# Rope as a delayed task, other delays in the solve, the fourth head's projections moved, products behind a norm run per token group, and w_mod moved into the FFN output

## The chip, the cores and the metric

The kernel runs on one core of one Trainium2 chip. The metric is the device time of one execution in microseconds. The engines are TensorE (PE; PEld is its weight load), VectorE (DVE), ScalarE (ACT), GpSimd (POOL) and SyncE (SP), which here only issues DMA transfers.

## The reference

A two-layer bidirectional encoder, run on two groups of 256 tokens with shared weights; the model width is 1024. The kernel holds both groups side by side as 512 token columns.

```python
def encoder_layer(x, c, cos, sin, p):
    sh1, sc1, gt1, sh2, sc2, gt2 = split(silu(c) @ p['w_mod'] + p['b_mod'], 6)
    h = rmsnorm(x, p['ln1_g']) * (1 + sc1) + sh1
    (q_down, kv_down, rg_x, rg_gate, gdn_qkv, gdn_z,
     gdn_alpha, gdn_beta, gates) = split_cols(h @ p['w_in'], IN_SPLITS)
    o_mla = mla_branch(...)     # latent attention, 8 heads, 32 rotary columns each
    o_rg  = rglru_branch(...)   # gated linear recurrence, both directions
    o_gdn = gdn_branch(...)     # chunked gated DeltaNet, 4 heads, both directions
    mixed = sum over n of sigmoid(gates[n]) * (o_n @ p['w_branch'][n])
    x = x + gt1 * (mixed @ p['w_out'])
    h2 = rmsnorm(x, p['ln2_g']) * (1 + sc2) + sh2
    u_lin, u_gate = split(dwconv_centred(h2 @ p['ffn_w_up'], ...), 2)
    return x + gt2 * ((silu(u_gate) * u_lin) @ p['ffn_w_down'])
# twice, then a final rmsnorm
```

In a DeltaNet head each chunk of 64 tokens needs the inverse of a unit lower triangular matrix, and then a short recurrence over the chunks.

## The kernel before

**Products.** Every large product takes float32 operands split into a high and a low part: `mm3` (L410) issues high by high, high by low and low by high into one PSUM bank. The weights lie in DRAM in *units* of 128x128, in the order of use, eight units to a *chunk* of 512 KB. `split_chunk` (L382) prefetches the chunk two further on, casts a loaded chunk to its high part on ACT (`wh`) and subtracts on DVE (`wl`); `unit` (L395) hands out one unit after the other and calls it six units ahead of a chunk's first use. There are four load buffers and two of each part. `gemm` (L416) makes one output row of 128 with all 512 token columns, or with 256 of one group; `gemms` (L425) makes three or six rows together. A row takes a bank of the PSUM pool `mm` (3 banks, L246); everything small, and three rows of every `gemms`, a bank of the pool `aux` (5 banks, L247).

**Order.** PE and SP run in the order in which the program is written; DVE, ACT and POOL are ordered by the framework. The program is written out by a planner: `Driver` (L141) counts a time of PE from the products issued. The list `BRANCHES` (L33) and `jobs` (L43) give the order of the large products; side tasks are generators that yield a delay of the table `SLACK` (L61) or an event, and after every unit `poll` runs those that are due. `until` waits for an event: it runs due tasks, then tasks from the list `spare`, and else moves the time on.

**Jobs.** `in6` makes the low-rank projections; `uq`, `uk`, `uv` the queries, keys and values of the attention; `gq.h`, `gk.h`, `gv.h`, `z.h` the DeltaNet projections of head h; `x`, `g`, `b` the recurrence; `gate.b.d` and `br.b.d` gate and output row d of branch b; then come the output projection (`out`), the FFN's `up` rows and the `down` rows.

**Rope.** `query` (L793) rotates rows 4 and 5 of the queries on DVE and at once writes on SP the transfer `drope` to DRAM and two transfers back into `Qt`; the event `ev_q`, for which the attention waits, follows 1.5 us later.

**The solve.** For each head `solve` (L1339) makes the decay and Gram products, writes the diagonal blocks out (`cb`, transfer `dl`), reads them into `Lb`, inverts them on POOL by 30 small steps (`xt`, `X`), writes them out (`dx`) and reads them into `W`. `combine` (L1452) then builds the inverse (`gdn_l`) and runs the recurrence (`gdn_rec`, `gdn_o`); it ends with a norm over `ssq` and `spread`. `combine` of a head begins after that of the head before (`ev_free`), and `gq.2` and `gq.3` wait for `ev_free` of two heads before.

**Norms.** `Norm` (L594) collects the squares as rows are finished. `scale` (L616) sums them on PE, takes the root on DVE and spreads it on PE into an `aux` bank that it holds while `modulated` (L582) reads it: DVE multiplies (`hn`, four buffers), ACT scales and shifts, POOL copies to the high part `hh`, DVE subtracts to the low part `hl`. Before the FFN and before the second layer the kernel waits for both groups' norms, runs the spare w_mod products meanwhile, makes all sixteen half tiles and then goes on with `up3` or `in6` over 512 columns. The last two output rows (`out` 6 and 7) and the last `down` row are made per group, group 0 first. The w_mod products of the second layer's first norm come in two lots (`ahead`, L1063): one paced through the `down` rows, one as spare work.

Of the kernel before, what the change touches and what calls it, by code (L numbers as in the profile page):

```python
# [1 line left out]

# [1 line left out]

# [21 lines left out]
AHEAD = 6  # L26
UC = 8

E2 = 0

# [6 lines left out]
    g.2 x.3 b.2.0 gate.1.2 b.2.1 gq.2 gk.2 gv.2 gate.1.3 g.3 b.3.0 gate.1.4 b.3.1 gate.1.5 gate.1.6  # L37
# [14 lines left out]

SIZE = {"in6": 48, "gq": 8, "gk": 8, "gv": 8, "uq": 3, "uk": 2, "pad": 2, "uv": 8,
        "gate": 8, "br": 4, "x": 8, "g": 8, "b": 2, "z": 8, "out3": 24, "out": 8, "up3": 24, "up": 8,
        "down": NFF, "close": 0, "mid": 0, "close2": 0}
JOBS = jobs()
NU = sum(SIZE[j[0]] for j in JOBS)
NCH = -(-NU // UC)
# [2 lines left out]
SLACK = {  # L61
    "modev": 0.7, "att_s": 3.2, "att_t": 1.8, "att_e": 1.0, "low_rank": 11.8, "low_rank_out": 152.5, "mla": 0.2,
# [3 lines left out]
    "rg_all": 16.0, "ssq": 6.5, "kq": 8.0, "norm": 2.8, "normed": 17.0, "mod1": 8.0, "mod2": 8.0,  # L66
    "kd": 0.1, "start": 0.6, "diag2": 4.6, "cq": 2.1, "lr_diag": 5.3, "diag": 30.4}


# [165 lines left out]
def _body(es, tc, nc, xT, cT, wall, wmod, pvec, fng, cst, rope, xinit, yT, dbg):  # L235
# [156 lines left out]
            sub(wl, raw, f32(wh))  # L392
            pieces[at] = (wh, wl)

    def unit():  # L395
        l, u = state["l"], state["u"]
        if u % UC == 0:
            split_chunk((l, u // UC))
            state["piece"] = pieces.pop((l, u // UC))
        elif (u + AHEAD) % UC == 0 and u + AHEAD < NU:  # L400
# [6 lines left out]
    def bank():  # L407
        return mm.tile([P, T], F32, name="mm_" + state["job"], tag="mm")

    def mm3(ps, w, x, first, last):  # L410
        PE.matmul(ps, w[0], x[0], start=first, stop=False)
        PE.matmul(ps, w[0], x[1], start=False, stop=False)
        PE.matmul(ps, w[1], x[0], start=False, stop=last)


    def gemm(xs, g=2):  # L416
# [177 lines left out]

    class Norm:
# [111 lines left out]

    for l in range(depth):
        state.update(l=l, u=0, job="in6")
        first = gemms(hs(h) if l else first_h(), 6)  # L710
        if not l:
            start.close()
            setup(0)
        pr = prm[l]

# [77 lines left out]
        def query(j):  # L793
            if j == 0:
                drv.until(ev_cq)
            ps = gemm(cq)
            if j < 4:
                A.activation(Qt[0:64, 2 * j, :], ps[0:64], AF.Copy, scale=96.0 ** -0.5)
                A.activation(Qt[0:64, 2 * j + 1, :], ps[64:128], AF.Copy, scale=96.0 ** -0.5)
                return  # L800
            cosq, sinq = rep2(rt_[:, 0, :]), rep2(rt_[:, 1, :])
            if j == 4:
                lr["rope"] = mp.tile([P, 4, T], F32, name="rope", tag="Vt")
            ab = lr["rope"][:, 2 * j - 8:2 * j - 6, :]
            mul(halves(ab[:, 0, :]), halves(ps), cosq)
            mul(halves(ab[:, 1, :]), halves(ps), sinq)
            if j == 5:
                x, y = lr["rope"][:, 0:2, :], ab
                sub(x[:, 0, :], x[:, 0, :], y[:, 1, :])
                add(x[:, 1, :], x[:, 1, :], y[:, 0, :])  # L810
                dr = dp.tile([P, 2, T], F32, name="drope", tag="drope")
                nc.sync.dma_start(dr, x)
                for e in range(2):
                    nc.sync.dma_start(Qt[64 + 16 * e:80 + 16 * e], dr.rearrange("(h p) e t -> e p h t", p=16)[e])
                ev_q.set(SLACK["rope"])

        def values():
            Vt = lr["Vt"] = mp.tile([P, 4, T], F32, name="Vt", tag="Vt")
# [182 lines left out]
                debug(f"x1_{d}_{l}", t)  # L1001


        def early(l, which, xs, sq, ks, h, pool):
            yield SLACK["norm"]
            yield from sq.scale(0)
            r = sq.r[0]
            for k in ks:
                x = xs[k]
                modulated(l, which, x[0] if isinstance(x, tuple) else x, r, k, 0, h, pool, 4)  # L1010


        def result(xs, sq, g):
# [47 lines left out]
            return tuple(half)  # L1061

        def ahead():  # L1063
            yield from modulation(l + 1, ((0, 1),), SLACK["mod2"], next_raw, 8)
            drv.spare.append([0.0, modulation(l + 1, ((2, 3),), 0.0, next_raw, 8)])


        last = l + 1 == depth
        for job in JOBS:
# [91 lines left out]
                    out_row(ps, d, 2)  # L1161
            elif k == "out":
                d, g = ix
                out_row(gemm(ms_, g), d, g)
                if (d, g) == (7, 0):
                    h2 = {}
                    drv.spawn(early(l, 1, x1, sq, range(E2), h2, op_))
                elif (d, g) == (7, 1):
                    wait(SLACK["norm"])
                    for us in sq.scale(1):  # L1170
                        wait(us)
                    for k in range(8):
                        for g in ((1,) if k < E2 else (0, 1)):
                            modulated(l, 1, x1[k], sq.r[g], k, g, h2, op_, 4)
                    wait(SLACK["normed"])
                    drv.drain_spare()
                    fill(op_, 2016)
                    ostack.close()
                    rstack.close()
                    fstack = ExitStack()  # L1180
                    fp = fstack.enter_context(tc.tile_pool(name="ffn", bufs=1))
            elif k == "up3":
                for n, ps in enumerate(gemms(hs(h2), 3)):
                    up(ps, n)
            elif k == "up":
                up(gemm(hs(h2)), ix[0])
            elif k == "down":
# [6 lines left out]
                        drv.spawn(ahead())  # L1194
                ps = gemm(acts, g)
                t = x1[d]
                for e in ((0, 1) if g == 2 else (g,)):
                    c = GS[e]
                    stt(t[:, c], ps[:, c], modA[:, 3, d, e:e + 1], t[:, c], ALU.mult, ALU.add)
                    if not last:  # L1200
                        nc.scalar.dma_start(xdram[:, d, c], t[:, c])
                sq.put(t, d, g)
                if g:
                    debug(f"x2_{d}_{l}", t)
                if last and d < 7:
                    A.activation(t, t, AF.Copy, scale=fg[:, d:d + 1])
                if (d, g) == (7, 0):
                    h = {}
                    drv.spawn(result(x1, sq, 0) if last else early(l + 1, 0, x1, sq, (), h, fp))
        if not last:  # L1210
            wait(SLACK["norm"])
            for us in sq.scale(1):
                wait(us)
            drv.drain_spare()
            for k in range(8):
                for g in range(2):
                    modulated(l + 1, 0, x1[k], sq.r[g], k, g, h, fp, 4)
            wait(SLACK["normed"])
        else:
            drv.spawn(result(x1, sq, 1))  # L1220
            drv.finish()
        fstack.close()


class GDN:
# [398 lines left out]
def pack(inp):  # L1624
# [11 lines left out]
    for l in range(depth):  # L1636
# [26 lines left out]
        for k, *ix in JOBS:  # L1663
# [14 lines left out]
            elif k == "up3":  # L1678
                w = side(up)
            elif k == "up":  # L1680
                w = up[ix[0]]
            elif SIZE[k] and k != "pad":
                w = seg[k][ix[0]]
            n = SIZE[k]
            if n and k != "pad":
                wall[l, u:u + n] = w.reshape(n, P, P)
            u += n

# [46 lines left out]
```

## Time and profile before

| | |
|---|---|
| median of 3 runs | 2016.12 us (2014.07 to 2019.35) |
| profiled execution | 2019.3 us, span 2017.5 us |
| PE busy | 1949.8 us, 97%, 11563 products |
| PEld busy | 1564.2 us, 78% |
| DVE busy | 1235.5 us, 61% |
| ACT busy | 823.9 us, 41% |
| POOL busy | 258.0 us, 13% |
| mean granted clock of PE | 0.986 |
| DMA | 231.44 MB, 115 GB/s |

Times are in microseconds from the start of the span. A view of waits says who waited for whom and how long in total; a timeline lists instructions with start and length, and in brackets the idle time ahead of one and what ended it; in a view of windows each engine has its busy time and, in brackets, its instructions, and the granted clock is a share of full speed. Lines such as L298 can be those of a helper, so the tile's name tells more than the line. Products are pipelined, so the length of one is more than the distance to the next.

### The profile page before, as it was taken

How to read it: one execution, taken by the hardware profiler on the slowest of the kernel's cores; microseconds unless marked ns; L12 is line 12 of the kernel's file. 1: busy time of each engine (PE TensorE's matmuls, PEld its weight loads, DVE VectorE, ACT ScalarE, POOL GpSimd, SP SyncE). 2: the span in 40 equal slices, each digit the busy share in tenths (PEclk: the TensorE clock that was granted, in tenths of full speed). 3: DMA queues.
4: the chain of work that ended last, by engine and by line, in shares of the span. 5: the costliest groups of instructions: out<-in, count | busy, mean ns of one | idle time of the engine just before them, and what ended most of it. 6: DMA issues, size and time to landing. Idle time of an engine off the chain costs nothing.

```text
span 2017.5 us, 29521 instructions
## 1 busy us (share of the span) xinstructions
PE 1949.8 (97%) x11563; PEld 1564.2 (78%) x11563; DVE 1235.5 (61%) x2324; ACT 823.9 (41%) x1275; POOL 258.0 (13%) x511
## 2 busy tenths in 40 slices
PE   9999999989999999999999999999898999999998
PEld 5777777768777888887877777777687888888887
DVE  5765776755456766652357758776553677676534
ACT  3444366523323544432234534655222344444322
POOL 1100162132200100000011004513130010000000
PEclk9999999999999999999999999999999999999999
DMA  8131443443325233353533123443432533333233
GB/s 318 63 115 53 111 129 113 122 129 94 92 97 186 95 94 104 95 178 106 192 121 94 63 74 113 120 141 110 124 76 74 214 100 94 96 96 100 94 97 102
DMA packets 141851, 231.44 MB, mean 115 GB/s; under 512 B 79760, under 2 KB 84240, under 8 KB 141712
## 3 DMA queue, kind: packets, MB, share of 16 engines
q1 hardware_dynamic: 136240, 221.95, 35.4%
q10 hardware_dynamic: 5472, 7.61, 1.1%
q8 instruction: 91, 1.49, 0.3%
q14 instruction: 48, 0.39, 0.1%
HBM read 221.66 MB, written 7.86 MB: 114 GB/s over the span
## 4 chain that ended last, share of the span: by engine, by line
PE 82%; DVE 5%; POOL 4%; DMA 4%; issue 2%; ACT 2%; SPq 2%; POOLq 0%; ACTq 0%; DVEq 0%
PE mm_up L220 24%; PE mm_down L220 12%; PE mm_gate L220 10%; PE mm_br L220 6%; PE mm_in L220 3%; PE mm_out L220 3%; PE mm_gk L220 2%; PE mod L220 2%; PE mm_gq L220 2%; POOL xt L292 2%; PE mm_gv L220 2%; POOL X L298 2%; PE att_s L220 1%; PE gdn_rec L220 1%; PE gdn_l L220 1%
## 5 line engine op out<-in xcount | busy, mean ns | idle before, releaser
L298 DVE TENSOR_TENSOR wl<-raw,wh 128x1024 fp32r<-128x1024 f32 x304 | 374.0, 1232 | 322.2 <-ACT wh L391 321.6
L391 ACT CAST wh<-raw 128x1024 fp32r<-128x1024 f32 x304 | 318.3, 1049 | 485.3 <-PE mm_down L220 127.9
L220 PE MATMUL mm_up<-hh,wh 128*128 128x512 f32 x704 | 275.8, 392 | 3.4 <-POOL hh L308 3.4
L220 PE MATMUL mm_up<-hl,wh 128*128 128x512 f32 x704 | 275.3, 391 | 0.0
L220 PE MATMUL mm_up<-hh,wl 128*128 128x512 f32 x704 | 275.1, 391 | 0.0
L301 DVE SCALAR_TENSOR_TENSOR cv<-mm_up,pv,cv 128x510 f32<-128x510 f32 x176 | 131.2, 748 | 61.3 <-ACT cv L571 58.0
L220 PE MATMUL mm_gate<-hh,wh 128*128 128x512 f32 x384 | 163.8, 427 | 0.3
L220 PEld LDWEIGHTS mm_up<-hh,wh 128*128 128x128 f32 x704 | 133.0, 189 | 31.6 <-POOL hh L308 3.9
L220 PEld LDWEIGHTS mm_up<-hl,wh 128*128 128x128 f32 x704 | 133.0, 189 | 28.0 <-DVE hl L298 0.3
L220 PEld LDWEIGHTS mm_up<-hh,wl 128*128 128x128 f32 x704 | 133.0, 189 | 27.6
L220 PE MATMUL mm_gate<-hl,wh 128*128 128x512 f32 x384 | 151.2, 394 | 0.0
L220 PE MATMUL mm_gate<-hh,wl 128*128 128x512 f32 x384 | 151.0, 393 | 0.0
L220 PE MATMUL mm_down<-ah,wh 128*128 128x512 f32 (+1 forms) x396 | 145.9, 369 | 0.0
L220 PE MATMUL mm_down<-ah,wl 128*128 128x512 f32 (+1 forms) x396 | 144.9, 366 | 0.6 <-DVE wl L298 0.6
L220 PE MATMUL mm_down<-al,wh 128*128 128x512 f32 (+1 forms) x396 | 144.7, 365 | 0.0
L308 POOL TENSOR_SCALAR hh<-hn 128x256 fp32r<-128x256 f32 x64 | 34.4, 549 | 663.8 <-ACT hn L588 661.2
L571 ACT ACTIVATE cv<-mm_up,pv 128x512 f32<-128x512 f32 x88 | 68.5, 780 | 88.9 <-PE mm_up L220 88.9
L220 PEld LDWEIGHTS mm_gate<-hh,wh 128*128 128x128 f32 x384 | 73.0, 190 | 22.2 <-issue 7.4
L220 PEld LDWEIGHTS mm_down<-ah,wh 128*128 128x128 f32 x396 | 74.7, 189 | 15.0 <-issue 3.3
L220 PEld LDWEIGHTS mm_gate<-hh,wl 128*128 128x128 f32 x384 | 72.7, 189 | 16.4
L220 PEld LDWEIGHTS mm_down<-ah,wl 128*128 128x128 f32 x396 | 74.7, 189 | 12.9 <-DVE wl L298 0.8
L220 PEld LDWEIGHTS mm_down<-al,wh 128*128 128x128 f32 x396 | 74.7, 189 | 11.9
(386 smaller groups left out, 3836.9 us busy)
## 6 DMA issues: line engine op xcount, KB each, us to landing
raw<-in_wall_dram SPq DMA_DIRECT2D x304, 512.0 KB, 3.6
raw<-in_wmod_dram SPq DMA_DIRECT2D x48, 512.0 KB, 3.6
mraw<-in_wmod_dram SPq DMA_DIRECT2D x16, 512.0 KB, 9.9
oraw<-in_wmod_dram SPq DMA_DIRECT2D x16, 512.0 KB, 6.6
hraw<-in_wmod_dram SPq DMA_DIRECT2D x32, 256.0 KB, 5.4
x<-in_xT_dram SPq DMA_DIRECT2D x8, 256.0 KB, 6.1
W<-dx SPq DMA_DIRECT2D x32, 64.0 KB, 3.0
xr<-in_xT_dram ACTq DMA_DIRECT2D x8, 256.0 KB, 3.7
```

Source lines behind the costliest of these rows:

```text
L220: return self.pe.matmul(out, lhsT, rhs, **kw)
L292: (eng or V).tensor_tensor(out, a, b, ALU.mult)
L298: (eng or V).tensor_tensor(out, a, b, ALU.subtract)
L301: V.scalar_tensor_tensor(out, a, s, b, op0, op1)
L308: G.tensor_scalar(hi, x, 1.0, 0.0, ALU.mult, ALU.add)
L391: A.copy(wh, raw)
L571: A.activation(dst, ps, AF.Identity, bias=bias, scale=w[lo])
```

## The change

- `BRANCHES`: `gq.3`, `gk.3` and `gv.3` stand directly behind `b.3.1`; the gates, branch rows and `z` around them are in another order.
- Delays of the solve: cb 4 to 5, dl 2.5 to 4, X 18 to 17, dx 3 to 5, W 3 to 4.
- Rope: the transfers are written by a spawned task, `drope` 6 us after the rotation, `Qt` 3 later, the event 4 later.
- Output rows 5, 6 and 7 (before: 6 and 7) are made per group, all of group 0 first; two jobs `pad2` fill the last chunk up, so that `up3` begins with a chunk.
- The new `gemms_behind` stands for `gemms` at `up3` and at `in6` of the second layer: its first 16 units are run over group 0's columns after that group's event, then over group 1's after the other event, and the rest over all columns. The task `behind` makes each group's norm and half tiles and sets the event.
- `modulated` has two instructions of DVE and one of ACT.
- The w_mod products of the second layer's first norm are all paced through the `down` rows, every 5 us (before: half of them, every 8 us).
- The last rows' additions for group 1 have priority, and the stores to `xdram` are written after the squares.

```diff
-    g.2 x.3 ... gate.1.4 b.3.1 gate.1.5 gate.1.6
-    br.1.0 br.1.1 gq.3 br.1.2 z.0 gk.3 br.1.3 gate.2.0 gv.3 gate.2.1 br.1.4 z.1 gate.2.2 br.1.5
-    gate.1.7 z.2 br.1.6 gate.2.3 gate.2.4 br.1.7 gate.2.5 z.3 gate.2.6 mid gate.2.7 br.2.0 br.2.1
+    g.2 x.3 ... gate.1.4 b.3.1 gq.3 gk.3 gv.3
+    gate.1.5 z.0 br.1.0 br.1.1 gate.1.6 br.1.2 br.1.3 gate.1.7 z.1 br.1.4 br.1.5 br.1.6 br.1.7 gate.2.0
+    gate.2.1 z.2 gate.2.2 gate.2.3 gate.2.4 gate.2.5 z.3 gate.2.6 mid gate.2.7 br.2.0 br.2.1
...
-    o += [("close2",), ("out3",)] + [("out", d, 2) for d in range(3, 6)]
-    o += [("out", 6, 0), ("out", 7, 0), ("out", 6, 1), ("out", 7, 1)]
+    o += [("close2",), ("out3",)] + [("out", d, 2) for d in range(3, 5)]
+    o += [("out", d, g) for g in range(2) for d in range(5, 8)]
+    o += [("pad2",)] * (-sum(SIZE[j[0]] for j in o) % UC // 2)
...
+    def gemms_behind(h, evs, n):
+        pss = [bank() if i < n - 3 else aux_tile(name="mm_" + state["job"]) for i in range(n)]
+        assert state["u"] % UC == 0 and EARLY == 2 * UC
+        us = [unit(False) for _ in range(EARLY)]
+        for g in range(2):
+            drv.until(evs[g])
+            c = GS[g]
+            for i, w in enumerate(us):
+                k, j = divmod(i, n)
+                mm3(pss[j][:, c], w, (h[k][0][:, c], h[k][1][:, c]), k == 0 and g == 0, False, skip_group_check=True)
+                drv.poll()
+                if g and i == UC - 1:
+                    split_chunk((state["l"], state["u"] // UC))
+        for i in range(EARLY, 8 * n):
+            k, j = divmod(i, n)
+            mm3(pss[j], unit(), h[k], False, k == 7, skip_group_check=True)
+            drv.poll()
+        return pss
...
-        mul(t, x[:, c], r)
-        A.activation(t, t, AF.Identity, bias=bias, scale=scale)
+        stt(t, x[:, c], scale, r, ALU.mult, ALU.mult)
...
-        split(t, h[k][0][:, c], h[k][1][:, c], pool=True)
+        hi = h[k][0][:, c]
+        A.activation(hi, t, AF.Identity, bias=bias)
+        stt(h[k][1][:, c], t, bias, f32(hi), ALU.add, ALU.subtract)
...
+                def place():
+                    yield SLACK["rope"]
                     dr = dp.tile([P, 2, T], F32, name="drope", tag="drope")
                     nc.sync.dma_start(dr, x)
+                    yield SLACK["rope_out"]
                     for e in range(2):
                         nc.sync.dma_start(Qt[64 + 16 * e:80 + 16 * e], dr.rearrange("(h p) e t -> e p h t", p=16)[e])
-                ev_q.set(SLACK["rope"])
+                    ev_q.set(SLACK["rope_in"])
+                drv.spawn(place())
...
+        def behind(l, which, xs, sq, g, h, pool, ev):
             yield SLACK["norm"]
+            yield from sq.scale(g)
+            r = sq.r[g]
+            for k in range(8):
                 x = xs[k]
+                modulated(l, which, x[0] if isinstance(x, tuple) else x, r, k, g, h, pool, 4)
+            ev.set(SLACK["h"])
...
         def ahead():
-            yield from modulation(l + 1, ((0, 1),), SLACK["mod2"], next_raw, 8)
-            drv.spare.append([0.0, modulation(l + 1, ((2, 3),), 0.0, next_raw, 8)])
+            yield from modulation(l + 1, ((0, 1), (2, 3)), SLACK["mod2"], next_raw, 8)
...
             elif k == "out":
                 d, g = ix
+                ps = gemm(ms_, g)
+                with tc.high_priority() if g == 1 else nullcontext():
+                    out_row(ps, d, g)
                 if (d, g) == (7, 0):
+                    h2, evs = {}, (drv.event(), drv.event())
+                if d == 7:
+                    drv.spawn(behind(l, 1, x1, sq, g, h2, op_, evs[g]))
+            elif k == "pad2":
+                unit(), unit()
             elif k == "up3":
+                pss = gemms_behind(h2, evs, 3)
+                drv.drain_spare()
```

## Rows read from the trace of the kernel before

**Rows 1.** Waits of PE, whole span: waiter, releaser, us total, times, longest

```profile
PE gdn_l L220 <- DMA W<-dx: 15.5, 6, 6.2
PE mm_uk L220 <- ACT wh L391: 9.6, 2, 4.8
PE spread L220 <- DVE onx L301: 4.6, 2, 2.3
PE ssq L220 <- DVE osq L295: 4.0, 2, 2.0
PE mm_up L220 <- POOL hh L308: 3.4, 2, 1.8
PE mm_gv L220 <- DVE wl L298: 2.8, 2, 1.4
...
PE gdn_rec L220 <- DVE r L295: 2.7, 2, 1.3
...
PE mm_in L220 <- POOL hh L308: 2.2, 2, 1.6
```

**Rows 2.** Waits of SP's queue, 60 to 125 us, same columns

```profile
SPq L812 <- DVE rope L298: 23.4, 1, 23.4
```

**Rows 3.** Timeline of ACT, 110 to 122 us: start, us, line, instruction, count

```profile
117.20 1.98 ACT L391 CAST wh<-raw 128x1024 fp32r<-128x1024 f32 x2
```

**Rows 4.** Windows: length, busy of five engines, granted clock, DMA share, GB/s

```profile
120.00:140.00 20.00, 20.00 (x88) 16.45 (x88) 11.79 (x42) 10.96 (x32) 0.00 (x0) 0.88 0.29 86
420.00:440.00 20.00, 13.83 (x179) 10.23 (x177) 6.91 (x11) 2.90 (x4) 2.46 (x9) 0.83 0.51 127
560.00:580.00 20.00, 16.17 (x70) 13.91 (x71) 9.50 (x21) 4.59 (x7) 0.00 (x0) 0.83 0.21 67
640.00:660.00 20.00, 17.53 (x135) 13.52 (x135) 16.25 (x57) 8.96 (x15) 5.54 (x11) 0.91 0.21 74
1100.00:1120.00 20.00, 15.03 (x59) 11.49 (x58) 9.62 (x12) 7.54 (x12) 0.00 (x0) 0.91 0.54 167
1420.00:1440.00 20.00, 17.91 (x273) 13.73 (x274) 6.99 (x11) 4.59 (x9) 4.68 (x12) 0.91 0.51 154
1540.00:1560.00 20.00, 13.68 (x82) 12.14 (x81) 7.53 (x21) 3.52 (x6) 0.00 (x0) 0.87 0.09 26
1640.00:1660.00 20.00, 18.33 (x72) 14.72 (x72) 15.37 (x38) 11.10 (x19) 8.32 (x15) 0.83 0.18 53
```

**Rows 5.** Timeline of PE: head 2 first and last, head 3 first

```profile
431.13 1.08 PE L220 MATMUL gdn_l<-W,B 32*32 32x32 f32 x64 [6.17 <-DMA W<-dx]
...
480.12 1.06 PE L220 MATMUL gdn_o<-E,v 128*128 128x128 f32 x8
...
523.10 0.74 PE L220 MATMUL gdn_l<-W,B 32*32 32x32 f32 x64 [0.69 <-DMA W<-dx]
```

**Rows 6.** Timeline of POOL: the same product in heads 0 and 2

```profile
251.41 0.45 POOL L292 TENSOR_TENSOR xt<-Lb,X 128x112 f32<-128x112 f32 x1
...
406.63 1.31 POOL L292 TENSOR_TENSOR xt<-Lb,X 128x112 f32<-128x112 f32 x1
```

**Rows 7.** Waits of SP's queue, 240 to 570 us

```profile
SPq L1408 <- DVE cb L1404: 38.0, 4, 20.1
```

**Rows 8.** Timeline of PE at the norm before the FFN, layer 0

```profile
637.72 0.28 PE L220 MATMUL mm_out<-ml,wh 128*128 128x256 f32 x1
637.84 0.28 PE L220 MATMUL mm_out<-mh,wl 128*128 128x256 f32 x1
...
641.46 2.80 PE L220 MATMUL mod<-oraw,csil 128*32 128x256 f32 x48
...
650.76 0.79 PE L220 MATMUL mm_up<-hh,wh 128*128 128x512 f32 x1 [1.77 <-POOL hh L308]
```

**Rows 9.** Groups by shape on DVE: count, busy us, mean ns, idle

```profile
L301 DVE SCALAR_TENSOR_TENSOR x<-mm_out,modA,xr 128x256 f32<-128x256 f32 x32 | 14.0, 478 | 14.5 <-PE mm_out L220 14.5
```

**Rows 10.** Chain of waits in order of time, 198 to 222 us

```profile
198.98 21.76 PE mm_br L220 x96
```

More of the change, by code (lines that the diff above doesn't have):

```diff
@@ L1 @@
-from contextlib import ExitStack
+from contextlib import ExitStack, nullcontext
 import numpy as np
@@ L27 @@
 UC = 8
-E2 = 0
+EARLY = 16
 BRANCHES = """
@@ L54 @@
         "gate": 8, "br": 4, "x": 8, "g": 8, "b": 2, "z": 8, "out3": 24, "out": 8, "up3": 24, "up": 8,
-        "down": NFF, "close": 0, "mid": 0, "close2": 0}
+        "down": NFF, "pad2": 2, "close": 0, "mid": 0, "close2": 0}
 JOBS = jobs()
@@ L63 @@
     "rg_x": 0.8, "ab": 5.7, "softplus": 13.7, "gates": 4.7, "v": 5.8, "ws": 3.0, "z": 0.2, "gw":
[2 rows of a table removed]
-    "rg_all": 16.0, "ssq": 6.5, "kq": 8.0, "norm": 2.8, "normed": 17.0, "mod1": 8.0, "mod2": 8.0,
[3 rows of a table added]
     "kd": 0.1, "start": 0.6, "diag2": 4.6, "cq": 2.1, "lr_diag": 5.3, "diag": 30.4}
@@ L393, in split_chunk, with unit @@
             pieces[at] = (wh, wl)
-    def unit():
+    def unit(ahead=True):
         l, u = state["l"], state["u"]
@@ L399, in unit @@
             state["piece"] = pieces.pop((l, u // UC))
-        elif (u + AHEAD) % UC == 0 and u + AHEAD < NU:
+        elif ahead and (u + AHEAD) % UC == 0 and u + AHEAD < NU:
             split_chunk((l, (u + AHEAD) // UC))
@@ L408, in bank, with mm3 @@
         return mm.tile([P, T], F32, name="mm_" + state["job"], tag="mm")
[L410 to L413, printed above, removed]
+    def mm3(ps, w, x, first, last, **kw):
+        PE.matmul(ps, w[0], x[0], start=first, stop=False, **kw)
+        PE.matmul(ps, w[0], x[1], start=False, stop=False, **kw)
+        PE.matmul(ps, w[1], x[0], start=False, stop=last, **kw)
     def gemm(xs, g=2):
@@ L709, in _body @@
         state.update(l=l, u=0, job="in6")
-        first = gemms(hs(h) if l else first_h(), 6)
+        first = gemms_behind(h, evs, 6) if l else gemms(first_h(), 6)
+        (fstack if l else start).close()
         if not l:
-            start.close()
             setup(0)
@@ L810, in query @@
                 add(x[:, 1, :], x[:, 1, :], y[:, 0, :])
[L811 to L814, printed above, removed]
-                ev_q.set(SLACK["rope"])
+                def place():
+                    yield SLACK["rope"]
+                    dr = dp.tile([P, 2, T], F32, name="drope", tag="drope")
+                    nc.sync.dma_start(dr, x)
+                    yield SLACK["rope_out"]
+                    for e in range(2):
+                        nc.sync.dma_start(Qt[64 + 16 * e:80 + 16 * e], dr.rearrange("(h p) e t -> e p h t", p=16)[e])
+                    ev_q.set(SLACK["rope_in"])
+                drv.spawn(place())
         def values():
@@ L1163, in _body @@
                 d, g = ix
-                out_row(gemm(ms_, g), d, g)
+                ps = gemm(ms_, g)
+                with tc.high_priority() if g == 1 else nullcontext():
+                    out_row(ps, d, g)
                 if (d, g) == (7, 0):
[L1166 to L1181, printed above, removed]
-            elif k == "up3":
-                for n, ps in enumerate(gemms(hs(h2), 3)):
+                    h2, evs = {}, (drv.event(), drv.event())
[3 more added lines that the diff above has]
+                unit(), unit()
+            elif k == "up3":
+                pss = gemms_behind(h2, evs, 3)
+                drv.drain_spare()
+                fill(op_, 2016)
+                ostack.close()
+                rstack.close()
+                fstack = ExitStack()
+                fp = fstack.enter_context(tc.tile_pool(name="ffn", bufs=1))
+                for n, ps in enumerate(pss):
                     up(ps, n)
@@ L1196, in _body @@
                 t = x1[d]
[L1197 to L1202, printed above, removed]
+                with tc.high_priority() if g == 1 else nullcontext():
+                    for e in ((0, 1) if g == 2 else (g,)):
+                        c = GS[e]
+                        stt(t[:, c], ps[:, c], modA[:, 3, d, e:e + 1], t[:, c], ALU.mult, ALU.add)
+                    sq.put(t, d, g)
+                if not last:
+                    for e in ((0, 1) if g == 2 else (g,)):
+                        nc.scalar.dma_start(xdram[:, d, GS[e]], t[:, GS[e]])
                 if g:
@@ L1207, in _body @@
                 if (d, g) == (7, 0):
[L1208 to L1222, printed above, removed]
+                    h, evs = {}, (drv.event(), drv.event())
+                if d == 7:
+                    drv.spawn(result(x1, sq, g) if last else behind(l + 1, 0, x1, sq, g, h, fp, evs[g]))
+    drv.finish()
+    fstack.close()
 class GDN:
@@ L1681, in pack @@
                 w = up[ix[0]]
-            elif SIZE[k] and k != "pad":
+            elif SIZE[k] and k[:3] != "pad":
                 w = seg[k][ix[0]]
             n = SIZE[k]
-            if n and k != "pad":
+            if n and k[:3] != "pad":
                 wall[l, u:u + n] = w.reshape(n, P, P)
```

7 lines of the change are left out of this document (1 added, 6 removed), and 5 rows, old and new, of the table SLACK.

## The prediction

> **What bounds the kernel now.** I read the waits of TensorE over the whole span first. PE is busy 97% of 2017.5 us, so a change can only win back PE's waits and the stretches in which its clock was low. The reader is to see that the waits are few, that each comes about once per layer, and that they sit in four places [rows 1]: solve products of the linear-attention heads waiting for `W` (15.5 us, six waits), `mm_uk` waiting for cast weights (9.6 us, two), the last head's tail (`gdn_rec` 2.7, `ssq` 4.0, `spread` 4.6, together 11.3 us), and the norm sites (`mm_up` 3.4, `mm_in` 2.2). Second, the granted clock in 20 us windows around those places [rows 4]: after each wait PE ran for a while at the lower of its two levels, 1.2 GHz. A mean of 0.88 over 20 us is 4.8 us at half speed, so 20 x (1 - 0.88) = 2.4 us lost if PE was busy; where PE also idled in the window I count about three quarters. Third, the timelines and SP's queue at each place.
>
> The sum is made against the profiled execution, 2019.3 us (span 2017.5 plus 1.8), and then moved to the median of the runs, 2016.1, which is 3.2 lower.
>
> **Rope.** The rotated queries leave by one `drope` transfer and return by two `Qt` transfers. SP is one queue in order: it stood 23.4 us at `drope` waiting for DVE's last rope instruction [rows 2], and every weight load emitted after it stood behind. The 14th weight chunk (units 104 to 111, first used by `uk.3`) was therefore cast only at 117.20, in one run with the next chunk [rows 3], and PE waited 4.8 us per layer. The change emits `drope` 6 us of the planner later (ten units on, about unit 92), `Qt` 3 later, the event 4 after that. So the loads of chunks 13 and 14, emitted at units 82 and 90, go ahead of all three transfers, and `drope` finds its data ready. The heads' attention is spawned only after `uv`, 32 units or 21.8 us of products later, so 13 us of delay costs nothing; without those products it would cost up to 11.5 us (13 less the 1.5 of before). Removed: 9.6 us of waits, and of 2.4 + 1.8 us of low clock [rows 4] at 120 and 1100 us some 3.8: 13.4. Late next is the chunk behind it: its buffer is free only when `gk.0` ends, and PE then has just two units of `uk.3` to run. Cast 1.0 and subtraction 1.2 us against 2 x 0.68 of products plus 0.68 inside `uv` leave 0.2 us at best; with a convolution ahead of them on ACT and DVE, 3. I take 1.5 per layer. Rope: **-10.4** (ends -13.4 and -7).
>
> **Longer delays in the solve.** cb, dl, dx, W go up by 1, 1.5, 2, 1, X down by 1: the combination is placed 4.5 us later in PE's order (35 instead of 30.5). PE waits there because it arrives before the data; products put ahead of it fill the wait. The longest is 6.17 [rows 5] and leaves 1.7; the other five share 9.3 us [rows 1], of which at most one can be as long and leave 1.7. Behind the waiting instruction PE has everything, in order. Removed with the clock (3.4 + 1.8, three quarters: 4 [rows 4] at 420 and 1420 us): 19.5. What the data themselves do is less sure. `dl` at 4 puts the `Lb` issues up to 1.5 us later in SP's order, and the three products moved up (next part) load DVE while POOL inverts the diagonal blocks. A POOL product of 128x112 took 0.45 us in the first head and 1.31 in the third, where DVE's subtraction of a weight chunk ran beside it [rows 6]. The Trainium skill has a rule for this (page "SBUF — State Buffer", section "Who interferes with whom"): a DVE instruction with two SBUF inputs and a GpSimd instruction that reads SBUF exclude each other for a whole instruction. The two rows agree. By the rule alone every additional chunk under the 30 POOL steps would hold them up by most of a microsecond, and two more chunks would leave 3.4 instead of 1.7 us of the longest wait. By the rows, one hold-up costs 1.31 - 0.45 = 0.86; I allow about 1 us at each of the two longest waits. Left: 3.4 + 2.1 = 5.5. Delays: **-14** (ends -19.5, and -5 if the data come later by as much as the products).
>
> **Fourth head earlier.** `gq.3` moves ahead of 24 units (gate.1.5, gate.1.6, br.1.0, br.1.1), `gk.3` of 36, `gv.3` of 48. A unit is three products of 0.2267 us [rows 10], so 16.3, 24.5 and 32.6 us. Head 3 begins its solve when its keys are there, and its combination needs head 2's end: that came at 481.2, and head 3 began at 523.10 [rows 5], so 42 us of room. With 24.5 less 4.5 it starts 20 us earlier, and the tail, which lay bare because only gate.2.7 was left, gets products beside it. The tail ran some 15 us, so 20 are enough. Removed: 11.3, and of 3.4 + 2.6 us of low clock [rows 4] at 560 and 1540 us 4.5: 15.8. Added: three projections in a row with their convolutions; the nearest row is the same run of head 2, where `mm_gv` waited 1.4 us for weights in each layer [rows 1]. Fourth head: **-13** (ends -15.8 and +2.8).
>
> **Norm sites.** Three sites change: `up3` in both layers, `in6` of layer 1. The first 16 units run first on group 0's tokens, then on group 1's. A half product takes 0.12 us [rows 8], two are 0.24 against 0.2267, so 48 pairs cost 0.64 us per site; the output row that is now split (24 pairs) costs 0.3 per layer; the padding units issue nothing. One weight chunk more per layer (153 for 152) lies beside products on ACT, DVE and SP; bare it would cost about 2.3. In `modulated` POOL's copy goes, ACT writes the high part, and DVE does two scalar_tensor_tensor instead of product and subtraction; the nearest row of that shape is 0.478 us [rows 9], so 0.96 a half tile, 7.7 us for eight.
>
> At `up3` I see a new wait. Small PSUM tiles have five banks. The first group's norm holds one until its eighth `hn` is read; `up3` takes three; the w_mod products that fill the gap take the fifth. The second group's norm is the sixth, and its products stand in PE's order right after the first half product, with the other half products queued behind them. Eight `hn` and four low parts (only four `hn` buffers) are 12 x 0.478 = 5.7 us, one chunk's subtraction 1.2, the weight split ahead of them about 2: ready some 8.7 us after the last output product, where PE arrives after 2.5. The site is then 8.7, 0.9 for the norm, 5.8 first halves, 1.8 w_mod and spread, 5.8 second halves, 5.4 for the last 8 units: 28.4. Before, 641.4 to 650.76 [rows 8] plus 72 x 0.2267 and 1.3 us of slow clock [rows 4] is 27.0. With a slow stretch after so long a wait I take +2 per site, +4. Without the bank wait it would be 23.7, or -3. `in6` has a free bank (its w_mod products, 4 us of PE either way, now run inside the FFN output every 5 us, their loads on SP one step at a time and 8 steps ahead), but nothing fills its gap: 2 us to the first `hh`, 2 to the second group's, against 2.2 for both groups before [rows 1] and slow first products: +1.5. Sites with the output rows: **+6** (ends -6 and +12, which is both banks waiting twice as long over). xdram's stores on ACT's queue move behind the squares and are read only by the output rows of the next layer: nothing.
>
> Sum: -10.4 - 14 - 13 + 6 = **-31.4**: 1987.9 for the profiled execution, **1985** on the median.
>
> **Rivals.** (1) No bank wait: the sites give 6 back instead of costing 6: **1973**. For it: only an allocation order is argued, no row shows a PSUM wait of this kind. 0.25. (2) The tail stays: head 3 is held by something other than its keys, and ends as late: 1985 + 15.8 = about **2000**. Against it the 42 us of room. 0.12. (3) Later transfers, same waits: rope and delays give half, -12 instead of -24: **1997**. For it: casts and `W` loads are placed by order, and order shifts everywhere. 0.13. (4) Slower: SP starves PE in the solve. SP stands at `dl` up to 20.1 us waiting for the blocks [rows 7], with weight loads behind; two heads now overlap in this queue. One such block cost 4.8 + 1.9 = 6.7 us at rope. There are eight solves; from the fifth (33.5) the gain is gone, with all eight the time is 1985 + 53.6 = about **2039**. Against it: with these blocks PE lost little there but the `W` waits [rows 1]. 0.05. The forecast has 0.45, with 1975 to 1995 as its own range.
>
> Range: 1964 (rival 1 with the better ends) to 2003 (rivals 2 and 3 in their middle). Within 0.3% (2010 to 2022) is about what cannot be told from no change. Faster 0.91, same 0.04 (upper parts of 2 and 3), slower 0.05.
>
> **What would show it.** Rope: no wait of SP at `drope`, the `mm_uk` wait gone, a short one at `mm_uv`. Delays: `gdn_l` from `W` under 6 us in total. Head: `ssq`, `spread`, `gdn_rec` waits gone, 0.83 at 560 gone; `mm_gv` twice per layer. Sites: a PE wait of about 6 us at `norm` by DVE `hn` just after the first `mm_up`; if it is missing, rival 1. It is wrong if the tail stays or if weight waits of several us stand in the solve.

## The result, and the profile after

The changed kernel takes 1995.1 us (median of 4 runs, 1993.7 to 1996.2) against 2017.7; the ratio is 0.9885, 95% interval 0.986 to 0.991. The forecast was 1985, with 1975 to 1995 as its own range, so the total came out at the slow end of it. Its terms were further off: the two that fill TensorE's waits in the solve and the tail gave 1.6 times what I wrote, one gave nothing, and the norm sites cost more than three times what I allowed.

The waits of PE over the whole span of the changed kernel come first (waiter, releaser, us in total, times, longest), against [rows 1].

```profile
PE mm_uk L221 <- ACT wh L392: 9.6, 2, 4.8
PE mm_up L221 <- DVE hn L302: 8.3, 2, 4.1
PE mm_out L221 <- DVE wl L299: 3.1, 4, 1.0
PE norm L221 <- DVE tsx L339: 2.7, 1, 2.7
PE ssq L221 <- DVE acc L296: 2.0, 1, 2.0
PE mm_in L221 <- ACT hh L614: 1.6, 1, 1.6
```

The 15.5 us for `W`, the tail (`spread`, `ssq` from `osq`, `gdn_rec`) and `mm_gv` are gone. The wait of `mm_uk` stands to the tenth as before. A new one, 4.1 us a layer, is at `mm_up`: it waits for DVE's `hn`.

SP's queue from 60 to 125 us, and ACT's timeline behind it (against [rows 2, 3]):

```profile
SPq L838 <- DVE rope L299: 23.8, 1, 23.8
```

```profile
117.08 0.63 ACT L1317 ACTIVATE kq<-gc 128x512 f32<-128x512 f32 x1 [2.44 <-DVE gc L302]
117.62 1.98 ACT L392 CAST wh<-raw 128x1024 fp32r<-128x1024 f32 x2
```

SP still stands at `drope`, and the two chunks behind it are still cast in one run at 117.6. SP's timeline (from 76 us) shows why: two loads, then `drope`, then `Qt`, the order of the kernel before, whose `drope` was issued at 102.14:

```profile
76.09 2.56 SPq L379 DMA_DIRECT2D raw<-in_wall_dram  x2
102.54 0.33 SPq L838 DMA_DIRECT2D drope<-rope  x1
105.13 0.80 SPq L841 DMA_DIRECT2D Qt<-drope  x2
```

Nothing moved. The windows (columns as in [rows 4]) where the clock was low before:

```profile
120.00:140.00 20.00, 20.00 (x89) 16.61 (x90) 12.38 (x42) 11.14 (x32) 0.00 (x0) 0.90 0.29 89
420.00:440.00 20.00, 20.00 (x232) 15.76 (x231) 11.00 (x19) 5.43 (x7) 0.29 (x1) 1.00 0.57 155
560.00:580.00 20.00, 20.00 (x90) 16.57 (x89) 16.18 (x23) 7.18 (x10) 0.00 (x0) 1.00 0.25 82
620.00:640.00 20.00, 15.41 (x138) 13.07 (x138) 12.52 (x37) 5.77 (x12) 0.00 (x0) 0.83 0.24 79
1100.00:1120.00 20.00, 19.03 (x75) 15.26 (x76) 11.74 (x36) 11.24 (x29) 0.00 (x0) 0.83 0.25 79
1540.00:1560.00 20.00, 20.00 (x90) 16.57 (x89) 17.03 (x26) 8.26 (x11) 0.00 (x0) 1.00 0.20 60
1600.00:1620.00 20.00, 14.85 (x126) 13.08 (x125) 13.78 (x40) 6.35 (x12) 0.00 (x0) 0.83 0.23 80
```

The solve (420) and the tail (560, 1540) run at the full clock; behind the wait of `mm_uk` it is still low (120 and 1100). The first norm site is worse (620: 0.83, where [rows 4] had 0.91 at 640); at the second the clock is the same (1600: 0.83), but PE is busy for less of it (14.85 us against 18.33). PE at the first of them (start, us, instruction, idle before):

```profile
621.73 2.80 PE L221 MATMUL mod<-oraw,csil 128*32 128x256 f32 x48
624.92 0.28 PE L221 MATMUL norm<-cs,acc 128*128 128x1 f32 x2
...
630.48 0.55 PE L221 MATMUL mm_up<-hh,wh 128*128 128x256 f32 x1 [4.15 <-DVE hn L302]
...
632.11 0.41 PE L221 MATMUL mm_up<-hl,wh 128*128 128x256 f32 x1
632.32 0.41 PE L221 MATMUL mm_up<-hh,wl 128*128 128x256 f32 x1
...
636.99 0.28 PE L221 MATMUL mm_up<-hl,wh 128*128 128x256 f32 x1
637.11 0.28 PE L221 MATMUL mm_up<-hh,wl 128*128 128x256 f32 x1
...
637.95 0.61 PE L221 MATMUL norm<-cs,tsx 128*128 128x128 f32 x4
```

The second group's norm (624.92) did not wait. The third row's first product did, 4.15 us, until the first group's last `hn` had been written (630.34). That it waited for a bank, the one with the norm that `hn` reads, is tested by e6. After it the half products came every 0.21 us until 635.7 instead of every 0.12, which is the clock's lower level (1.2 GHz for 2.4), and because of both the second group's scale was spread only at 637.95. DVE then stood idle before the second group's first product (DVE's timeline):

```profile
629.47 0.87 DVE L302 SCALAR_TENSOR_TENSOR hn<-x,modA,norm 128x256 f32<-128x256 f32 x2
...
638.60 1.26 DVE L302 SCALAR_TENSOR_TENSOR hn<-x,modA,norm 128x256 f32<-128x256 f32 x3 [6.34 <-PE norm L221]
```

To see where time went I cut each profiled execution at products that all versions have (us between starts of products, read from the groups of one tile each):

| stretch | before | after | e3 | e4 | e8 | e9 | e11 | e12 |
|---|---|---|---|---|---|---|---|---|
| first `mm_br` to first `mm_out`, layer 0 | 396.3 | 374.5 | 374.1 | 374.1 | 374.1 | 374.3 | 374.2 | 374.6 |
| the same, layer 1 | 396.4 | 374.5 | 374.7 | 374.0 | 374.2 | 374.5 | 374.1 | 374.2 |
| first to last `mm_out`, layer 0 | 46.1 | 48.0 | 46.1 | 46.1 | 46.1 | 46.1 | 46.1 | 46.1 |
| last `mm_out` to last `mm_up`, layer 0 | 250.2 | 254.8 | 250.3 | 249.5 | 256.1 | 251.5 | 248.8 | 248.4 |
| the same, layer 1 | 251.1 | 254.9 | 251.7 | 250.1 | 256.6 | 250.7 | 250.4 | 250.4 |
| last `mm_up`, layer 0, to last `mm_in`, layer 1 | 172.3 | 177.7 | 172.2 | 174.3 | 174.7 | 174.3 | 176.9 | 174.5 |
| last `mm_in` to first `mm_uv`, layer 1 | 50.4 | 50.5 | 50.4 | 43.8 | 43.7 | 43.8 | 43.7 | 43.8 |

From before to after: the two first rows -43.7 (I had -27 for delays and head), `mm_uk` 0 (rope, -10.4), and the rest +19.7 (+6): output rows +1.9 and +1.8, `up3` +4.6 and +3.8, `in6` +5.4, 1.1 between the first `mm_uv` and the first `mm_br` of layer 1, and 1.0 in the last layer's FFN output. Together -24, as the spans say: 2017.5 to 1993.6.

How far can one execution be trusted? Two stretches that hold the same instructions in several kernels tell. Up to the first `mm_in` of layer 0 the kernel before took 25.3 us at a mean clock of 0.93, but e1 and e2 (described below), the same up to there, 23.1 us at 1.00; the changed kernel took 24.6 us at 0.93, but e6 and e7, the same as it up to there, 22.7 and 23.0 us at 1.00. And e1 and e2, whose `in6` is that of the kernel before, took 174.5 and 173.5 us in the last stretch but one, against its 172.3: over 10 us from the first `mm_in` of layer 1 their clock was 0.73 and 0.83, and 1.00 in the kernel before. So some 2 us of the 5.4 at `in6` can be a clock that the kernel before happened to keep.

### The profile page after: what moved, and what is told of

It reads as the page before. It is cut to its first block, busy times and chain, and to the rows that moved or that the text cites. A ratio compares the mean times of both kernels' runs of the same rounds, so it can differ in the third digit from the quotient of the medians.

```text
span 1993.6 us, 29836 instructions
## 1 busy us (share of the span) xinstructions
PE 1947.4 (98%) x11755; PEld 1569.9 (79%) x11755; DVE 1238.6 (62%) x2328; ACT 813.2 (41%) x1279; POOL 216.1 (11%) x447
## 4 chain that ended last, share of the span: by engine, by line
PE 89%; DVE 6%; DMA 2%; POOL 1%; ACT 1%; issue 1%; SPq 0%; DVEq 0%; ACTq 0%; POOLq 0%
PE mm_up L221 24%; PE mm_down L221 12%; PE mm_gate L221 12%; PE mm_br L221 7%; PE mm_out L221 3%; PE mm_in L221 3%; PE mod L221 3%; PE mm_gq L221 2%; PE mm_z L221 2%; PE mm_gk L221 2%; PE mm_g L221 2%; PE att_s L221 2%; PE mm_gv L221 1%; PE mm_x L221 1%; PE gdn_l L221 1%; PE gdn_rec L221 1%
## 5 line engine op out<-in xcount | busy, mean ns | idle before, releaser
L221 PE MATMUL mm_up<-hh,wh 128*128 128x512 f32 (+1 forms) x736 | 282.8, 384 | 8.3 <-DVE hn L302 8.3
L221 PE MATMUL mm_up<-hh,wl 128*128 128x512 f32 (+1 forms) x736 | 282.0, 383 | 0.5 <-DVE wl L299 0.5
L221 PE MATMUL mm_up<-hl,wh 128*128 128x512 f32 (+1 forms) x736 | 281.9, 383 | 0.0
L221 PEld LDWEIGHTS mm_up<-hh,wh 128*128 128x128 f32 x736 | 140.9, 191 | 35.5 <-issue 9.5
L221 PEld LDWEIGHTS mm_up<-hh,wl 128*128 128x128 f32 x736 | 140.8, 191 | 27.5 <-DVE wl L299 1.4
L221 PEld LDWEIGHTS mm_up<-hl,wh 128*128 128x128 f32 x736 | 140.9, 191 | 26.1
L221 PEld LDWEIGHTS mm_gate<-hl,wh 128*128 128x128 f32 x384 | 72.5, 189 | 11.7
L768 POOL TENSOR_SCALAR Kt<-Kt 32x512 f32<-32x512 f32 x14 | 10.6, 756 | 638.4 <-DVE Kt L296 561.6
```

What stands on the lines that cost most here:

```text
L221: return self.pe.matmul(out, lhsT, rhs, **kw)
L768: G.tensor_scalar(Kt[64:96, hd, :], Kt[64:96, 0, :], 1.0, 0.0, ALU.mult, ALU.add)
```

## The experiments

All ratios are to the kernel before, run on the same chip; times are medians. A difference between two kernels, worked out from their ratios, is uncertain by some 4 us, and by some 6 us against the changed kernel.

**One part alone.** e1 takes only the delays, e2 only the order, e3 both, on the kernel before.

```
e1, e3:  -"cb": 4.0, "dl": 2.5, "X": 18.0, "dx": 3.0, "W": 3.0
         +"cb": 5.0, "dl": 4.0, "X": 17.0, "dx": 5.0, "W": 4.0
e2, e3:  -gate.1.5 gate.1.6 br.1.0 br.1.1 gq.3 br.1.2 z.0 gk.3 br.1.3 gate.2.0 gv.3 ...
         +gq.3 gk.3 gv.3 gate.1.5 z.0 br.1.0 br.1.1 gate.1.6 br.1.2 br.1.3 ...
```

> The kernel before with only the longer solve delays (cb 5, dl 4, X 17, dx 5, W 4); the fourth head, the norm sites and the rope transfers stay as before. Theory: products fill the wait for W, so gdn_l from W falls from 15.5 us to under 6 and some of the slow clock behind it goes: -14 us (-19.5 at best), about 2003. Rival A: head and delays only work together, since the data come later by what the products take: -5, about 2012. Rival B: the 44 us that the stretch from the first branch row to the first output row lost in the two layers came mostly from the head: delays alone give under -8.

Measured: 2004.5, ratio 0.9927 (0.9911 to 0.9944), -15 us. The theory held, and `W` waits 2.9 us in total. But the runs lie between 1999.4 and 2009.0; the profiled one, 2000.4, is among the lowest, and its stretches give 19.8.

> The kernel before with only the fourth head's three projections moved ahead in the order of the work. Theory: the tail's waits (ssq, spread, gdn_rec, 11.3 us) and the low clock at 560 and 1540 us go, two short waits of mm_gv come: -13 us, about 2004; the waits for W stay near 15.5 us. Rival: the tail stays because something else than the keys holds head 3: 0 to +3, about 2018.

Measured: 1989.6, ratio 0.9861 (0.9847 to 0.9875), -28 us, twice what I had, and two parts of the theory are plainly wrong, as the waits of e2 show:

```profile
PE mm_uk L220 <- ACT wh L391: 9.6, 2, 4.8
PE gdn_l L220 <- DMA W<-dx: 5.0, 4, 2.3
...
PE mm_x L220 <- ACT gt L910: 2.8, 2, 1.7
PE mm_gv L220 <- DVE wl L298: 2.8, 2, 1.4
```

The tail's three waits are gone, as said. The two further waits of `mm_gv` did not come: the two in the list are head 2's, as before, and the fourth head waits instead at `gdn_tr`, for `kq`, 0.97 and 0.92 us. And `W` fell as well, from 15.5 to 5.0 us, without any longer delay. The granted clock is whole behind the tail; in e2's windows (columns: length, PE busy, clock, DMA share, GB/s):

```profile
560.00:580.00 20.00, 20.00 (x90) 1.00 0.16 53
1540.00:1560.00 20.00, 20.00 (x90) 1.00 0.20 57
420.00:440.00 20.00, 18.36 (x295) 1.00 0.56 152
```

> The kernel before with the head's move and the longer delays, norm sites and rope transfers as before. Theory: between the same two markers the whole change gained 21.8 us per layer, so this kernel runs 44 us shorter, about 1974, some 20 us below the whole change; the difference is what the norm sites cost. Rival: part of those 44 us belongs to the norm sites' changes (the output row that is split lies outside, but weight chunks and the rows' priority act earlier): 1980 to 1990.

Measured: 1977.2, ratio 0.9791 (0.9778 to 0.9804), -42 us. The theory held: this part of the change is 19 us faster than the whole change by the ratios, so the rest of the change costs what it lost. By the stretches e1 gave 19.8, e2 30.1 and both 43.9: 6 us are counted in either, since both take the wait for `W` (12.6 and 10.5 of its 15.5 us).

**Rope, truly late.** In the changed code the placing waits 6 us of the planner, but right behind it the planner's clock jumps: the next job, `uk.0`, waits for the low-rank event, whose delay is 152.5. The 6, 3 and 4 us all pass in this jump, before another chunk's load is emitted, and SP's order is that of the kernel before. e4 (on e3) and e5 (on the changed kernel) hang the placing on an event that is set behind `gq.0`:

```
-                    yield SLACK["rope"]
+                    yield ev_place
...
                 drv.spawn(gdn.part(k[1], ix[0], gemm(hs(h))))
+                if (k, ix[0]) == ("gq", 0):
+                    ev_place.set(0.0)
```

> As the one with head and delays, and the transfers of the rotated queries are placed only after the first product of head 0's queries (gq.0), so that the loads of two more weight chunks stand ahead of them in SP's queue; Qt follows 3 us of planner time later. Theory (the rope step as I meant it): SP's wait of 23 us at drope goes, the mm_uk wait of 4.8 us per layer goes with most of its slow clock: 12 us less than without it, about 1962. Rival: the cast was late by ACT's own order (kq and the convolutions ahead of it), not by the load: the mm_uk wait stays and the time is the same within 2 us.

Measured: 1963.3, ratio 0.9724 (0.9711 to 0.9737), 13.5 us below e3 by the ratios. SP's queue (60 to 125 us) and PE's waits of e4:

```profile
SPq L815 <- DVE rope L298: 8.9, 1, 8.9
```

```profile
PE mm_up L220 <- POOL hh L308: 3.5, 2, 1.8
...
PE mm_uv L220 <- ACT Vt L842: 1.3, 2, 0.7
```

SP's timeline of e4 (from 76 us): one load more stands ahead of `drope`, and another ahead of `Qt`:

```profile
77.76 14.78 SPq L378 DMA_DIRECT2D raw<-in_wall_dram  x3
101.55 0.33 SPq L815 DMA_DIRECT2D drope<-rope  x1
101.97 0.38 SPq L378 DMA_DIRECT2D raw<-in_wall_dram  x1
104.44 0.80 SPq L818 DMA_DIRECT2D Qt<-drope  x2
```

`mm_uk` is gone from the list, and `mm_uv` waits 0.7 us a layer, for ACT. So the rival is out: the load was what came late.

> The changed kernel, with the transfers of the rotated queries placed only after gq.0's product instead of 6 us of planner time after the rope instructions. Theory: in the changed kernel the delays of 6, 3 and 4 us all pass inside one jump of the planner's clock (the wait for the low-rank event with its 152.5 us), so nothing moved; moved past the loads, they give what they gave with the head and the delays alone: the mm_uk wait (9.6 us) and its slow clock go, -13 to -14 us against the changed kernel, ratio to before about 0.982. Rival: with the changed kernel's other orders the wait only moves to uv: -5, ratio 0.986.

Measured: 1979.5, ratio 0.9797 (0.9783 to 0.9811), -17.8 against the changed kernel by the ratios. In the profiles the stretch from the last `mm_in` to the first `mm_uv` fell by 6.7 us in each layer, 13.4 together; 2.2 more came ahead of the first `mm_in`, where the clock was 1.00 against 0.93; the intervals hold the rest. The rope step was right about the mechanism and wrong about the code that should bring it.

**The norm sites on the changed kernel.** e6 gives `up3`'s first row a bank of the large pool, e7 orders the output rows as before, e10 takes the old `modulated`.

```
e6:  -pss = [bank() if i < n - 3 else aux_tile(...) for i in range(n)]
     +pss = [bank() if i < max(n - 3, 1) else aux_tile(...) for i in range(n)]
e7:  -[("out", d, 2) for d in range(3, 5)], [("out", d, g) for g in range(2) for d in range(5, 8)]
     +[("out", d, 2) for d in range(3, 6)], [("out", d, g) for g in range(2) for d in range(6, 8)]
e10: -stt(t, x[:, c], scale, r, ...); A.activation(hi, t, bias); stt(lo, t, bias, hi, ...)
     +mul(t, x[:, c], r); A.activation(t, t, bias, scale); split(t, hi, lo, pool=True)
```

> The changed kernel, with up3's first row in a bank of the large PSUM pool instead of the small one, so that the tile of the second group's norm or of the third row no longer waits for the eighth hn of the first group. Theory: the two waits of mm_up for hn (8.3 us) and most of the slow clock behind them go: -10 us against the changed kernel, ratio to before about 0.983. Rival A: DVE's chain is the limit, PE only waits a little later, for the second group's hl: -3, ratio 0.987. Rival B: the waits for the bank move to another tile: 0.

Measured: 1986.6, ratio 0.9837 (0.9823 to 0.9851), -9.7. In the profiles `up3` gives 2.2 and 3.8 of it; 1.9 more came ahead of the first `mm_in`, which the edit does not touch, with the clock. The wait for `hn` is gone, so the bank was it; in its place PE waits later and less:

```profile
PE mm_up L221 <- DVE wl L299: 6.1, 4, 2.8
```

> The changed kernel with the output rows ordered as before (rows 6 and 7 alone split by token group, row 5 whole). Theory: the stretch of the output rows took 48.0 us instead of 46.1 per layer because of the third split row; 1.9 comes back there, but the norm of the first group has one half row less as cover, 2.9 us: +1 per layer, ratio to before 0.9895. Rival: the cover was not needed, since PE waits later for the bank in any case: -4 us, 0.9865.

Measured: 1988.2, ratio 0.9843 (0.9829 to 0.9857), -8.5: the rival. The output rows give 1.6 and 1.8 back, and `up3` 1.6 and 1.3; as in e6, 1.6 more lies ahead of the first `mm_in`, with the clock. Behind them the planner reaches the first product with all w_mod products done, and PE's bank wait is 3.3 instead of 4.1 us: the third split row covered nothing.

> The changed kernel with the old modulated (product on DVE, scale and bias on ACT, high part by POOL, low part on DVE). Theory: in the changed kernel a chunk's subtraction already stands in the middle of the first group's half tiles, so the new modulated costs nothing there: the same within 3 us, ratio 0.987 to 0.99. Rival: the 13.7 us that the new modulated cost alone are in the changed kernel's norm sites too (they cost 20 us in all): -10, ratio 0.9835.

Measured: 1998.9, ratio 0.9891 (0.9868 to 0.9913): the same, and the rival is out. In the changed kernel the new `modulated` doesn't cost what it costs alone. The sum hides differences: with the old one `up3` took 3.9 and 2.4 us longer, and the first `mm_br` of layer 0 came 3.3 us earlier, 1.5 of it ahead of the first `mm_in`, with the clock.

**The new `modulated` alone.** e8 puts it into e4, e9 puts e8's weight chunks first:

```
+            with tc.high_priority() if state["job"] in ("up3", "in6") else nullcontext():
                 A.copy(wh, raw)
                 sub(wl, raw, f32(wh))
```

> The kernel before with the head's move, the delays and the late rope transfers, and of the norm sites only the new modulated (two scalar_tensor_tensor on DVE, the high part written by ACT, no POOL copy); products wait for both norms as before. Theory: the chain to the first hh is one instruction shorter, so the waits of mm_up and mm_in for POOL's hh (5.7 us) fall by about 1 to 1.5 us a site: -3 to -4 us against the same kernel without it (1963), about 1960. Rival: DVE now carries the product and the low part for sixteen half tiles, and the products run dry behind the first: +3, about 1966.

Measured: 1974.6, ratio 0.9776 (0.9762 to 0.979), 10.5 slower than e4. The chain to the first `hh` is shorter, as the theory has it (1.1 us of wait instead of 1.8), but PE ran dry later. The waits of e8 at the first site, 600 to 680 us:

```profile
PE mm_up L220 <- DVE wl L298: 3.4, 1, 3.4
PE mm_up L220 <- ACT hh L592: 1.1, 1, 1.1
```

DVE's timeline in e4 and then in e8 shows why. In e4 the first chunk's subtraction stands at 625.66, in the middle of the half tiles; in e8 the first two stand together behind the last of them:

```profile
625.00 0.75 DVE L292 TENSOR_TENSOR hn<-x,norm 128x256 f32<-128x256 f32 x2
625.66 1.22 DVE L298 TENSOR_TENSOR wl<-raw,wh 128x1024 fp32r<-128x1024 f32 x1
627.17 2.01 DVE L298 TENSOR_TENSOR hl<-hn,hh 128x256 fp32r<-128x256 f32 x4 [0.30 <-POOL hh L308]
```

```profile
633.08 1.28 DVE L301 SCALAR_TENSOR_TENSOR hl<-hn,modT,hh 128x256 fp32r<-128x256 f32 x3 [0.63 <-ACT hh L592]
634.28 2.35 DVE L298 TENSOR_TENSOR wl<-raw,wh 128x1024 fp32r<-128x1024 f32 x2
```

> The kernel with the head's move, the delays, the late rope transfers and the new modulated (1974.6, 13.7 us of span above the same kernel with the old modulated), and the cast and the subtraction of weight chunks put ahead of the norm's half tiles in the order of ACT and DVE at up3 and in6. Theory: the new modulated does not cost by its own work on DVE (13.7 us of hn and hl against 13.2 at a site) but by the order: the first subtraction of a chunk comes behind the last half tiles at 634.3 instead of 625.7, so up3 runs dry once (3.4 us a layer) and then runs slow. With the chunk first, -8 us: about 1966, ratio 0.973. Rival: the clock fell in the gap ahead of the first product (0.52 in 5 us) and would fall again: that part, 2.5 us a layer, stays, and the waits move to hh: -2, ratio 0.9765.

Measured: 1963.5, ratio 0.9714 (0.969 to 0.9738). The wait for `wl` is gone and the time is that of e4: what the new `modulated` cost was the place of the weight chunks in the order of DVE (and of ACT, which the edit moves too), not its work. Half of the rival is true all the same: the clock did fall again (0.58 from 621 to 626 us), and the wait for `hh` stayed at 1.1.

**All repairs.** e11 is the changed kernel with e5, e6, e7 and the weight chunks first; e12 is e11 with `in6` as before the change (its second w_mod half back in the gap).

> The changed kernel with the three repairs together (rope transfers behind gq.0, up3's first row in the large pool, rows as before with only 6 and 7 split) and the weight chunks first at up3 and in6. Theory: the repairs add up (-16, -10, -8 alone against the changed kernel), and the last waits of mm_up and mm_in for a chunk (7.4 us) shrink: about 1960, ratio 0.970. Rival: bank and rows remove the same wait once, and the chunk first only delays the half tiles: about 1969, ratio 0.975, worse than the kernel with order, delays and rope alone (0.9724).

Measured: 1961.5, ratio 0.971 (0.9686 to 0.9733).

> The kernel with all repairs (1961.5), and in6 of the second layer as before the change: its products wait for both norms, the second half of the w_mod products fills the gap behind the FFN output, and the products of the FFN output take it no more. Theory: the w_mod products cost 7.3 us inside the FFN output and nothing in the gap, the gap grows by as much, and the wait of in6 for the second group's high parts with its slow clock goes: the stretch from the last mm_up to the last mm_in falls from 176.9 to 174 us, so -3: about 1958, ratio 0.9695. Rival: with the weight chunks first and the new modulated the gap behind the FFN output is longer than in the kernel before: 0 to +2, ratio 0.971 to 0.972.

Measured: 1961.0, ratio 0.9711 (0.9696 to 0.9727). The stretch of `in6` fell by 2.4 us, from 176.9 to 174.5, but the runs can't tell the two kernels apart. Both beat the changed kernel by 35 us and the kernel before by 58. That they are better than e4, which has none of the norm sites' changes, isn't shown: the intervals overlap.

## Why the prediction was right in sum and wrong in its terms

The total is near partly by luck: delays and head gave 16.7 us more than I wrote, and that made up for most of the 10.4 us of rope that did not come and the 13.7 us that the norm sites cost beyond my 6.

- **What bounds.** Right. PE's waits and low clock were what could be won, and each clear gain above came with a wait of PE that went or shrank.
- **Rope, -10.4: failed, at 0.** The step "the change emits `drope` 6 us of the planner later (ten units on, about unit 92)" converted planner time into units at the products' rate. The planner does not run at that rate where a job waits for an event: there it jumps to the event, here past all three delays. I had the delay of 152.5 before me. With the placing tied to a product (e4, e5) the term is -13.5, the end I gave as its best, and the 1.5 us that I put down as late next measured 0.7 a layer, and for ACT's `Vt`, not for the chunk. SP's wait at `drope`, which I said would go, was still 8.9 us, without harm.
- **Delays, -14: right.** Alone -15 (19.8 in the profiled execution). The wait for `W` left 2.9 us in e1 and none beside the moved head, where I left 5.5. The hold-up of POOL by DVE, for which I kept 2.1 us back, went on: in the changed kernel a product of 128x88 took 1.30 us in the third head and 0.40 in the fourth. With the longer delays PE no longer waited for `W`.
- **Fourth head, -13: mis-sized, at -28 alone.** The mechanism was right (head 3 begins its combination at 484.8 instead of 523.1 in e2, and the tail's waits leave). Three terms were off. I gave the wait for `W` to the delays alone, though the move takes 10.5 of its 15.5 us. I counted three quarters of the slow clock behind the tail; it all went. And the 2.8 us that I added for `mm_gv` were 1.9 at `gdn_tr` in e2, and 0.4 in the changed kernel.
- **Norm sites, +6: mis-sized, at +19.7.** The bank wait is there, 4.1 us where I had about 6, at the third row and not at the norm. I had let it cost +2 a site, because it takes the place of a gap of 9.4 us before. What I left out is behind it: 24 half products at 0.21 instead of 0.12 us (2.2 us), which with the wait hold back the spread of the second group's scale, so that DVE stood 6.3 us for it and the second half products began 3.2 us after the spread where I had 1.8. (The 23.7 us that I gave for a site without the bank wait do not follow from its terms; 28.4 less 6.2 is 22.2.) `up3` cost 8.4 for 4. The output rows cost 3.7 for 0.6, with waits for weights (3.1 us against 1.1 before, and 1.0 in e7 without that split) at the chunk more that I had priced at nothing beside products. `in6` cost 5.4 for 1.5, some 2 of which can be the clock (see the stretches above), and the 1.1 in the attention behind it I can't place. Its w_mod half takes 7.3 us inside the FFN output (137.0 against 129.7 from the last `mm_up` to the last `mm_down`), where I had 4 either way, and the gap it left shrank by just as much (9.7 to 2.3); so the change at `in6` wins nothing and keeps the waits for the second group.
- **Rivals.** (1), no bank wait, is out: the wait is there. (2) is out: the tail left. (3) gave nearly the right time (1997) for a wrong reason: rope gave nothing, but the delays gave all of theirs. (4) is out: PE's waits for weights and blocks in the solve are two of 0.6 us, at `mm_b`.

What stays open: why the order alone shortens the wait for `W`. In e2 PE came to it some 3 us later and the data a little earlier, counted from the first branch row, but I didn't separate the two. And the 2.4 us between e11 and e12 at `in6` are read from one execution each.

## What to carry to other kernels

A delay in a planner's units moves work only if the planner's clock runs evenly there; where something is to be placed behind certain loads, tie it to the job that emits them, and compare the order of the queue before counting a gain. Work put into a gap that already hides other work is not free twice: price what the gap held before (here w_mod products), where it goes, and what stands behind the new wait. Several waits that one edit can reach should be summed once for the pair of edits and not shared out, since either may take them.

## What the runs showed of the hardware that I had not expected

The same gap can cost the clock or not. In e4 and in e8 PE did the same work up to it, in the same places (48 w_mod products, a norm, 16 more, a wait of 0.70 us). But e8's clock was down before the last wait: its spread at 618.75 took 1.03 us, that of e4 0.69. In windows of 5 us (busy of PE, its weight loads, DVE, ACT, POOL, then the clock) e4 kept the full clock, although PE was busy less in the first window:

```profile
616.00:621.00 5.00, 2.53 (x29) 1.75 (x20) 4.37 (x23) 1.96 (x5) 0.98 (x3) 1.00 0.01 3
621.00:626.00 5.00, 5.00 (x22) 3.96 (x22) 4.49 (x13) 3.81 (x8) 2.53 (x6) 1.00 0.00 0
```

and e8 fell to the lower level:

```profile
616.00:621.00 5.00, 3.18 (x31) 2.22 (x30) 4.28 (x22) 1.66 (x4) 0.00 (x0) 0.79 0.05 17
621.00:626.00 5.00, 5.00 (x12) 3.73 (x13) 4.81 (x13) 1.95 (x5) 0.00 (x0) 0.52 0.00 0
```

In e9 it fell too (0.58 in the second window). The price here is 22 against 12 products in 5 us, about 2.3 us, and a sum made from PE's idle time alone would not have told the two apart. The exception is e4's first layer: in the 5 us from the first `mm_up` product the mean clock was 0.50 to 0.71 in both layers of the kernel before, of e1, e2 and e3, and in e4's second layer. All this is one execution each; what decides it isn't shown.
